# Layer 1's experts: a branch on TensorE to products that work on 32 slots, for experts with 32 tokens or fewer

## The chip, the cores and the metric

The kernel runs on one core of a Trainium2 chip. The metric is the device time of one execution in microseconds; less is better. A core has TensorE (PE in the profile, and PEld for its weight loads), VectorE (DVE), ScalarE (ACT), GpSimd (POOL), SyncE (SP, which issues most DMAs) and 16 DMA engines. They run beside each other and wait for each other by semaphores.

## The reference, cut to what matters

The model has two layers. Each mixes 256 latent tokens with 256 context tokens (attention beside a linear recurrence), and then sends tokens through 16 experts, of which a router picks two for each token. In layer 1, the last, only the 256 latent tokens go through the experts, so an expert has 32 tokens on average.

```python
D_MODEL = 1024
N_EXPERTS = 16
TOP_K = 2
D_EXPERT = 512
...
def grouped_moe(h, router_w, router_b, w_gate, w_up, w_down):
    ...
    out = jnp.zeros_like(h)
    for e in range(N_EXPERTS):
        hid = jax.nn.silu(h @ w_gate[e]) * (h @ w_up[e])
        out = out + combine[:, e:e + 1] * (hid @ w_down[e])
    return out
```

Everything is fp32. Each expert has three weights of 2048 KB (gate and up 1024 x 512, down 512 x 1024), and each layer has weights of its own.

## The kernel before

Layer 0's experts (`experts`) give every expert 64 slots, and up to three extra blocks of 32 slots each that PE and GpSimd reach through branches on the expert's token count (`extras`, line 1572). The products of an extra block (`upx`, `downx`) have 128x32 stationary operands and 256 moving columns, four beside each other in the array; their PSUM tiles are `ccg` and `ccd`.

Layer 1's experts (`experts_last`) have no extra blocks: every expert works on 64 slots, whatever its count, and tokens beyond 64 would go through a loop behind the stage (`more`). `route` puts each token's rank within its expert into `rk`. For an expert e these steps follow each other:

- `one_hot_f` (DVE, line 1723) compares ranks with slot numbers and makes a 0/1 matrix of tokens by slots, for two experts at a time.
- `gat0` (PE, tile `pgx`): products of the tokens with these matrices gather the two experts' tokens, transposed, into `xT`.
- `up` (PE, tile `pgu`): gate goes to partitions 0 to 63, up to partitions 64 to 127, 8 products of 512 columns each. Two beside each other fill the array's 128 columns.
- `gated`: ACT makes silu of gate, DVE multiplies by up (tile `hid`).
- `hturn` (PE, tile `phd`) turns `hid`, ACT copies it out.
- `down` (PE, tile `pdn`): 8 products of 512 columns, the two halves of the output beside each other.
- `gain` and `halves` (DVE, ACT) scale the result and split it into two parts for the return; `oturn` (PE, tile `poh`) turns the 0/1 matrix.
- `back` (PE, tile `pcb`, and DVE): four products bring the slots back to tokens, and DVE adds them into `xtok` with the combine weight.

The order on each engine is written out by hand in `step` and run as written (`manual_schedule`): up of expert e + 1, down of e, and back of e - 1 between their parts. The pieces of up and of back are interleaved: after the fifth and sixth of the eight steps of up comes one back, after the last another, and the same within down.

The weights come through SP's queue (`load`, line 216) into eight buffers of 2048 KB, so 2 2/3 experts fit. The loads are issued in the order gate, up, down, expert by expert, and each waits until PE has done the last product that reads the buffer it takes. Gate and up have 16 KB of one partition in one run in memory, and so has layer 1's down; layer 0's down has four runs of 4 KB. Expert 15's gate and up are loaded in two halves each.

One fp32 product is two records on PE in the trace. All products stand at line 114 (`mm`), so they are told apart by their tiles.

Of the kernel before, what the change touches and what calls it, by code (L numbers as in the profile page):

```python
# [108 lines left out]
def backbone(ctx: ExitStack, tc: tile.TileContext, a: dict):  # L109
# [99 lines left out]
    def part(l, e, i, pl=None):  # L209
        n_, k = (("gate", 8), ("up", 8), ("down", 4))[i]  # L210
        t = wchunk(f"w{n_[0]}{l}_{e}", pl).rearrange("p (k n) -> p k n", k=k)

        return t, a[f"exp_w_{n_}"][l, e].rearrange("(k p) n -> p k n" if i == 2 and l == 0 else "(p k) n -> p k n", k=k)
# [1060 lines left out]
    def route(l, lg, Q, R):  # L1274
# [72 lines left out]
        if last:  # L1347
            return
# [361 lines left out]
    def experts_last(l, tmp, h2k, ahead, after):  # L1710


        r = rt_all[l]
        rk, oi, wc = r["rk"], r["oi"], r["wc"]
        xt, hid, hidT, oh, ohT, hl, W = {}, {}, {}, {}, {}, {}, {}
        it = C("iota")[:, 0:64]

        def one_hot_f(es, rks):

            o = tmp.tile([P, 2, 2, 64], F32, name="ohf", tag="ohf", bufs=3)  # L1720
            for i, e in enumerate(es):
                for t in range(2):
                    dve.tensor_scalar(o[:, i, t, :], it, rks[i][t], None, op0=OP.is_equal)
                oh[e] = o, i

# [14 lines left out]
        def up(ps, x, w, ks):  # L1740
            for k in ks:
                mm(ps[0:64, :], x[:, k, :], w[0][:, k, :], k == 0, k == KC - 1)
                mm(ps[64:128, :], x[:, k, :], w[1][:, k, :], k == 0, k == KC - 1)

        def gated(ps):
# [3 lines left out]
            dve.tensor_tensor(h.rearrange("s k p -> s p k"), sg.rearrange("s (p k) -> s p k", k=4),  # L1749
                              ps[64:128, :].rearrange("s (p k) -> s p k", k=4), op=OP.mult)  # L1750
            return h
# [9 lines left out]
        def down(ps, h, w, ks=range(4)):  # L1761
            for k in ks:
                for q in range(2):
                    mm(ps[64 * q:64 * q + 64, :], h[:, k, :], w[2][:, k, q * 512:(q + 1) * 512], k == 0, k == 3)

# [35 lines left out]
        def step(e):  # L1801
# [22 lines left out]
        def more():  # L1824
# [3 lines left out]
            with tc.If(anyv > 0, preferred_fallthrough_block=False):  # L1828
                for e in range(NE):
                    ov = nc.values_load(oi[0:1, e:e + 1], min_val=0, max_val=8)  # L1830
                    with tc.If(ov > 0, preferred_fallthrough_block=False):
# [5 lines left out]
                        with tc.For_i(0, ov, 1):  # L1837
                            rb = tmp.tile([P, 2], F32, name="rbg", tag="rbg", bufs=1)
                            dve.tensor_scalar(rb[:], rk[:, :, e], base[:, 0:1], None, op0=OP.subtract)
                            one_hot_f((e,), [[rb[:, t:t + 1] for t in range(2)]])  # L1840
                            gat0((e,))
                            ps = psb("pgu", "mm")
                            up(ps, xt[e], w, range(KC))
# [15 lines left out]
        with tc.manual_schedule(engines=ORDERED):  # L1859
# [11 lines left out]
            pu, pd = psb("pgu", "mm"), psb("pdn", "mm")  # L1871
# [4 lines left out]
            for i in range(3):  # L1876
                up(pu, xt[e], W[e], ((0, 1, 2, 3, 4), (5, 6), (7,))[i])
                if i < 2:
                    back2(e - 2, i)
            hid[e] = gated(pu)  # L1880
            for i in range(2):
                down(pd, hidT[e - 1], W[e - 1], (2 * i, 2 * i + 1))
                back2(e - 2, 2 + i)
# [3 lines left out]
            pd = psb("pdn", "mm")  # L1887
            down(pd, hidT[e], W[e])
# [11 lines left out]
    MOE = dict(mm=2, tr=2), dict(mm=3, tr=3, cb=2)  # L1900
# [124 lines left out]
```

## Time and profile before

| | |
|---|---|
| median of 3 runs | 1109.69 us (1105.55 to 1113.52) |
| the profiled execution, its own time | 1107.49 us |
| its span in the profile | 1105.6 us |
| PE busy | 984.8 us, 89% |
| DVE busy | 600.5 us, 54% |
| ACT busy | 432.3 us, 39% |
| POOL busy | 195.7 us, 18% |
| DMA, mean rate over the span | 270 GB/s |
| first and last pgu products of layer 1 | 843.6 and 1073.4 us |

The profile is one execution. The span goes from the first to the last instruction; the execution's own time is 1.9 us longer. Times in rows are microseconds from the span's start unless marked ns. Busy time of PE counts matmuls in the array; PEq and PEld are its queue and its weight loads. "x <- y" in a row of waits means that x waited for y.

### The profile page before, as it was taken

How to read it: one execution, taken by the hardware profiler on the slowest of the kernel's cores; microseconds unless marked ns; L12 is line 12 of the kernel's file. 1: busy time of each engine (PE TensorE's matmuls, PEld its weight loads, DVE VectorE, ACT ScalarE, POOL GpSimd, SP SyncE). 2: the span in 40 equal slices, each digit the busy share in tenths (PEclk: the TensorE clock that was granted, in tenths of full speed). 3: DMA queues.
4: the chain of work that ended last, by engine and by line, in shares of the span. 5: the costliest groups of instructions: out<-in, count | busy, mean ns of one | idle time of the engine just before them, and what ended most of it. 6: DMA issues, size and time to landing. Idle time of an engine off the chain costs nothing. (4 is left out here: it accounts for less than half of the span.)

```text
span 1105.6 us, 15540 instructions
## 1 busy us (share of the span) xinstructions
PE 984.8 (89%) x5791; PEld 520.2 (47%) x5791; DVE 600.5 (54%) x1363; ACT 432.3 (39%) x858; POOL 195.7 (18%) x208
## 2 busy tenths in 40 slices
PE   5999999899589989999898599897977999999993
PEld 3555465678444434333332366353765434444431
DVE  3567487686743325534433356679863344444445
ACT  3635678465511212212221264796741122221222
POOL 2000033331544313212110200205241000000000
PEclk9999999899669989999998799998997999999996
DMA  9947674011866876999997565558156799999941
GB/s 381 396 167 299 229 272 186 30 39 58 323 244 259 286 287 190 398 407 410 395 397 305 155 268 188 200 180 305 49 210 270 317 421 413 429 400 416 397 197 41
DMA packets 51963, 298.87 MB, mean 270 GB/s; under 512 B 5457, under 2 KB 8401, under 8 KB 35969
## 3 DMA queue, kind: packets, MB, share of 16 engines
q1 hardware_dynamic: 44800, 279.88, 64.1%
q0 software_dynamic: 6896, 16.87, 5.4%
q8 instruction: 73, 1.20, 0.4%
q10 hardware_dynamic: 144, 0.52, 0.1%
q14 instruction: 50, 0.40, 0.1%
HBM read 288.86 MB, written 10.49 MB: 271 GB/s over the span
## 5 line engine op out<-in xcount | busy, mean ns | idle before, releaser
L114 PE MATMUL pdn<-wd,hidT 128*64 128x512 f32 x512 | 124.3, 619 | 5.3 <-PEq L1572 4.0
L114 PE MATMUL pgu<-wg,xgT 128*64 128x512 f32 x256 | 118.7, 617 | 0.3 <-issue 0.3
L114 PE MATMUL pgu<-wu,xgT 128*64 128x512 f32 x256 | 118.7, 617 | 0.2 <-DMA wu<-exp_w_up_dram 0.2
L114 PE MATMUL pgu<-wu,xT 128*64 128x512 f32 x256 | 116.5, 598 | 0.0
L114 PE MATMUL pgu<-wg,xT 128*64 128x512 f32 x256 | 116.5, 598 | 0.0
L1795 DVE SCALAR_TENSOR_TENSOR xtok<-pcb,wc,xtok 128x512 f32<-128x512 f32 x64 | 47.7, 750 | 102.7 <-PE pcb L114 102.7
L1455 DVE TENSOR_TENSOR hid<-hid,pgu 64x512 f32<-64x512 f32 x16 | 11.0, 690 | 126.2 <-ACT hid L1454 126.2
L114 PE MATMUL pproj<-hh,wps 128*128 128x512 f32 x288 | 76.9, 407 | 0.0
L846 POOL TENSOR_TENSOR wo<-wf,wo 128x512 fp32r<-128x512 f32 x29 | 41.0, 1434 | 201.9 <-ACT wo L844 170.1
L1430 POOL DMA_INDIRECT yd<-xtok,sgs x24 | 38.6, 1608 | 185.0 <-DVE xtok L1489 183.5
L114 PEld LDWEIGHTS pdn<-wd,hidT 128*64 128x64 f32 x512 | 34.7, 140 | 67.5 <-issue 66.8
L114 PEld LDWEIGHTS pgu<-wg,xgT 128*64 128x64 f32 x256 | 34.8, 142 | 65.2 <-issue 64.7
L114 PEld LDWEIGHTS pproj<-hh,wps 128*128 128x128 f32 x288 | 53.2, 188 | 19.6 <-issue 6.5
L114 PEld LDWEIGHTS pgu<-wg,xT 128*64 128x64 f32 x256 | 32.5, 136 | 61.6 <-issue 60.7
L1454 ACT ACTIVATE hid<-pgu 64x512 f32<-64x512 f32 x16 | 9.4, 590 | 104.8 <-PE pgu L114 104.7
L1954 POOL TENSOR_TENSOR fin<-xtok,fin 128x512 f32<-128x512 f32 x2 | 2.5, 1278 | 254.8 <-DVE xtok L1795 254.8
L1748 ACT ACTIVATE hid<-pgu 64x512 f32<-64x512 f32 x16 | 9.4, 589 | 94.6 <-PE pgu L114 94.5
L795 ACT ACTIVATE Pm<-psc,mx,qy 128x512 f32<-128x512 f32 (+1 forms) x48 | 33.5, 703 | 21.3 <-DVE mx L789 21.1
L497 DVE TENSOR_TENSOR wps<-win,wps 128x512 fp32r<-128x512 f32 x48 | 32.6, 687 | 14.9 <-ACT wps L496 14.4
L114 PE MATMUL pproj<-hT,wps 128*128 128x512 f32 x144 | 39.8, 397 | 0.0
L114 PEld LDWEIGHTS pgu<-wu,xgT 128*64 128x64 f32 x256 | 34.8, 142 | 6.9 <-issue 5.2
L114 PE MATMUL pwa<-wo,mh 128*128 128x512 f32 x128 | 36.3, 407 | 1.6 <-POOL wo L846 0.9
(442 smaller groups left out, 2079.5 us busy)
## 6 DMA issues: line engine op xcount, KB each, us to landing
wd<-exp_w_down_dram SPq DMA_DIRECT2D x31, 2048.0 KB, 14.2
wu<-exp_w_up_dram SPq DMA_DIRECT2D x27, 2048.0 KB, 9.6
wg<-exp_w_gate_dram SPq DMA_DIRECT2D x27, 2048.0 KB, 15.9
xtok<-ada_w_dram SPq DMA_DIRECT2D x7, 2048.0 KB, 7.4
win<-w_in_dram SPq DMA_DIRECT2D x6, 2048.0 KB, 16.2
adac<-ada_w_dram SPq DMA_DIRECT2D x5, 2048.0 KB, 8.0
xtok<-ada_w_dram SPq DMA_DIRECT2D x8, 1024.0 KB, 5.1
adac<-ada_w_dram SPq DMA_DIRECT2D x8, 1024.0 KB, 4.9
```

Source lines behind the costliest of these rows:

```text
L114: pe.matmul(out, lhsT, rhs, start=start, stop=stop)
L497: dve.tensor_tensor(wl, wv, wh.bitcast(F32), op=OP.subtract)
L795: act.activation(ps[h], sc_[i][h], AF.Exp, bias=mx[:, h:h + 1], scale=qr[:, ti, j, h:h + 1], accum_out=sm[:, h:h + 1])
L846: pool.tensor_tensor(lo, w, hi.bitcast(F32), op=OP.subtract)
L1430: st = pool.indirect_dma_start(out=dst, out_offset=bass.IndirectOffsetOnAxis(ap=idx, axis=0), in_=y, in_offset=None, bounds_check=dst.shap ...
L1454: mark.append(act.activation(sg, ps[0:64, :], AF.Silu).ins.name)
L1455: dve.tensor_tensor(h.rearrange("s k p -> s (k p)"), sg, ps[64:128, :], op=OP.mult)
L1748: act.activation(sg, ps[0:64, :], AF.Silu)
L1795: dve.scalar_tensor_tensor(x, cb, wc[:, t, e:e + 1], x, op0=OP.mult, op1=OP.add)
L1954: (dve if q else pool).tensor_tensor(fin["t"][:, 1 + t, cs], x, fin["t"][:, 0, cs], op=OP.mult)
```

## The change

- `route` makes, for layer 1, a flag for every expert that is 1 when it has over 32 tokens (`big`, and as an integer `bigi`): two small DVE operations.
- `one_hot_f` compares ranks with slot numbers chosen by the flag: 1 to 64 for a big expert, and 1 to 32 twice for another, so that each of its tokens has two slots, s and s + 32. One more DVE operation for each expert, two at the start of the stage (`its`).
- `either` loads the flag into a register of PE (once for an expert) and branches, for up and for down. Only PE branches.
- The other arm of up (`up_half`) multiplies 32 slots by 256 columns, four products beside each other: the first and second half of gate, the first and second half of up. A token's first 256 hidden values then stand in slot s, the other 256 in slot s + 32.
- The other arm of down (`down_half`) sums over 256 hidden values for each slot, so that a token's result is the sum of its two slots; `back` adds them, as the 0/1 matrix has both.
- For that, the down weights of layer 1 have the row order of layer 0's (runs of 4 KB), and `gated` writes in plain order.
- All of up now stands in one tile, `pgu`, with one buffer, cleared once by ACT; the four `back` of an expert are no longer between the parts of up and of down but behind each.

```diff
@@ part
-        return t, a[f"exp_w_{n_}"][l, e].rearrange("(k p) n -> p k n" if i == 2 and l == 0 else "(p k) n -> p k n", k=k)
+        return t, a[f"exp_w_{n_}"][l, e].rearrange("(k p) n -> p k n" if i == 2 else "(p k) n -> p k n", k=k)
@@ route
         if last:
+
+            big = rt_all[l]["big"] = R.tile([P, NE], F32, name="big", tag="big", bufs=1)
+            bigi = rt_all[l]["bigi"] = R.tile([P, NE], I32, name="bigi", tag="bigi", bufs=1)
+            dve.tensor_scalar(big[:], cnt[:], 0.5 * NB, None, op0=OP.is_gt)
+            dve.tensor_copy(bigi[:], big[:])
             return
@@ experts_last
+        its = tmp.tile([P, 2, 64], F32, name="its")
+        dve.tensor_scalar(its[:, 0], C("iota")[:, 128:192], float(NB), None, op0=OP.subtract)
+        dve.tensor_tensor(its[:, 1], it, its[:, 0], op=OP.subtract)
+
+        def one_hot_f(es, rks, own=True):
 
             o = tmp.tile([P, 2, 2, 64], F32, name="ohf", tag="ohf", bufs=3)
             for i, e in enumerate(es):
+                ie = it
+                if own:
+                    ie = tmp.tile([P, 64], F32, name="ite", tag="ite", bufs=2)[:]
+                    dve.scalar_tensor_tensor(ie, its[:, 1], big[:, e:e + 1], its[:, 0], op0=OP.mult, op1=OP.add)
                 for t in range(2):
-                    dve.tensor_scalar(o[:, i, t, :], it, rks[i][t], None, op0=OP.is_equal)
+                    dve.tensor_scalar(o[:, i, t, :], ie, rks[i][t], None, op0=OP.is_equal)
                 oh[e] = o, i
+
+        def either(e, whole, half):
+
+            if e not in bv:
+                bv[e] = nc.values_load(bigi[0:1, e:e + 1], engines=[PEe], min_val=0, max_val=1)
+            with tc.If(bv[e] > 0, preferred_fallthrough_block=False) as c:
+                whole()
+            with c.Else():
+                half()
...
+        def up_half(ps, x, w):
+
+            for k in range(KC):
+                for m in range(2):
+                    for q in range(2):
+                        mm(ps[64 * m + 32 * q:64 * m + 32 * q + 32, 0:256], x[:, k, 0:32], w[m][:, k, 256 * q:256 * q + 256],
+                           k == 0, k == KC - 1)
...
+        def down_half(ps, h, w):
+
+            for k in range(2):
+                for q in range(2):
+                    for i in range(2):
+                        mm(ps[64 * q + 32 * i:64 * q + 32 * i + 32, :], h[:, k, 32 * i:32 * i + 32],
+                           w[2][:, 2 * i + k, q * 512:(q + 1) * 512], k == 0, k == 1)
+
+        pgu = psb("pgu", "gu")
+        act.activation(pgu, C("iota"), AF.Copy, scale=0.0)
+
+        def ups(e):
+            ps = pgu
+            either(e, lambda: up(ps, xt[e], W[e]), lambda: up_half(ps, xt[e], W[e]))
+            return ps
...
@@ step
-            pu = psb("pgu", "mm")
-            for i in range(3):
-                up(pu, xt[e + 1], W[e + 1], ((0, 1, 2, 3), (4, 5), (6, 7))[i])
-                if e >= 1 and i:
-                    back(e - 1, 0, i - 1)
-            hid[e + 1] = gated(pu)
+            hid[e + 1] = gated(ups(e + 1))
+            if e >= 1:
+                for i in range(2):
+                    back(e - 1, 0, i)
             if e >= 0:
-                pd = psb("pdn", "mm")
+                pd = downs(e)
+            if e >= 1:
                 for i in range(2):
-                    down(pd, hidT[e], W[e], range(2 * i, 2 * i + 2))
-                    if e >= 1:
-                        back(e - 1, 1, i)
+                    back(e - 1, 1, i)
```

The last expert's order is changed in the same way, and the PSUM buffers from three that `pgu` and `pdn` share to two for `pdn` and one for `pgu`.

## Rows read from the trace of the kernel before

**Rows 1.** Page, part 2: DMA share in tenths and GB/s, 40 slices.

```profile
DMA  9947674011866876999997565558156799999941
GB/s 381 396 167 299 229 272 186 30 39 58 323 244 259 286 287 190 398 407 410 395 397 305 155 268 188 200 180 305 49 210 270 317 421 413 429 400 416 397 197 41
```

**Rows 2.** Windows: us, busy us of each engine, PEclk, DMA share, GB/s.

```profile
851.00:861.00 10.00, 7.25 (x44) 6.21 (x46) 1.71 (x2) 2.58 (x4) 0.00 (x0) 0.83 0.94 374
861.00:872.00 11.00, 11.00 (x56) 3.70 (x54) 1.75 (x2) 2.08 (x5) 0.00 (x0) 1.00 0.51 186
872.00:1063.00 191.00, 191.00 (x929) 76.32 (x927) 84.43 (x132) 39.57 (x81) 0.00 (x0) 1.00 0.99 411
1063.00:1064.00 1.00, 1.00 (x6) 0.29 (x4) 0.56 (x1) 0.00 (x0) 0.00 (x0) 1.00 0.54 221
```

**Rows 3.** Timeline of PE: start us, us, engine, line, operation, count.

```profile
859.53 0.64 PE L114 MATMUL pgu<-wg,xT 128*64 128x512 f32 x1
...
866.45 3.60 PE L114 MATMUL pdn<-wd,hidT 128*64 128x512 f32 x16
...
887.64 0.64 PE L114 MATMUL pgu<-wg,xT 128*64 128x512 f32 x1
...
917.92 0.64 PE L114 MATMUL pgu<-wg,xT 128*64 128x512 f32 x1
```

**Rows 4.** Waits of SP's queue, 780:1106: us in total, times, longest us.

```profile
SPq L216 <- PE pgu L114: 105.7, 9, 15.8
SPq L216 <- PE pdn L114: 93.1, 13, 12.9
```

**Rows 5.** Windows of two stretches with the load queue full.

```profile
572.80:582.00 9.20, 8.40 (x50) 3.67 (x48) 5.11 (x10) 2.73 (x6) 1.55 (x1) 1.00 1.02 411
922.00:937.00 15.00, 15.00 (x66) 4.63 (x61) 6.76 (x12) 2.89 (x6) 0.00 (x0) 1.00 1.01 431
```

**Rows 6.** Timeline of PE near the end.

```profile
1052.37 0.64 PE L114 MATMUL pgu<-wg,xT 128*64 128x512 f32 x1
...
1079.34 3.65 PE L114 MATMUL pdn<-wd,hidT 128*64 128x512 f32 x16
```

**Rows 7.** Groups by form, PE, 300:640: count | busy us, mean ns.

```profile
L114 PE MATMUL ccg<-wu,xxT 128*32 128x256 f32 x256 | 28.6, 380 | 0.0
...
L114 PE MATMUL ccd<-wd,hixT 128*32 128x256 f32 x256 | 14.8, 381 | 0.0
```

**Rows 8.** Line 1572: durations in ns min/median/max, first and last start us.

```profile
L1572 PEldq COMPARE_BRANCH  x66: 69/218/3558, 323.5 to 615.9; - x66
```

**Rows 9.** Waits of PE, 300:620: us in total, times, longest us.

```profile
PE pslot L114 <- PEq L1572: 4.2, 10, 0.7
...
PE phd L1461 <- PEq L1572: 3.8, 7, 0.7
```

**Rows 10.** Line 1828, columns as in rows 8.

```profile
L1828 PEldq COMPARE_BRANCH  x2: 84/1910/3736, 1089.9 to 1090.6; - x2
```

**Rows 11.** Timeline of DVE before layer 1's experts.

```profile
837.77 0.73 DVE L1723 TENSOR_SCALAR ohf<-cst,rk 128x64 f32<-128x64 f32 x4
```

**Rows 12.** Timeline of PE; in brackets the idle us before, and its releaser.

```profile
838.44 5.19 PE L114 MATMUL pgx<-ohf,h2k 128*128 128x128 f32 x32 [1.12 <-DVE ohf L1723]
...
853.75 0.46 PE L1756 MATMUL phd<-ident,hid 64*128 64x64 f32 x4 [3.10 <-DVE hid L1749]
854.13 5.47 PE L114 MATMUL pgx<-ohf,h2k 128*128 128x128 f32 x32
...
883.97 3.74 PE L114 MATMUL pgx<-ohf,h2k 128*128 128x128 f32 x32
```

**Rows 13.** Timeline of SP's queue: issues of weight loads.

```profile
850.67 0.33 SPq L216 DMA_DIRECT2D wd<-exp_w_down_dram  x1
...
866.64 0.33 SPq L216 DMA_DIRECT2D wu<-exp_w_up_dram  x1
```

**Rows 14.** Window after the idle time at 853, columns as in rows 2.

```profile
855.00:858.40 3.40, 3.40 (x18) 3.40 (x17) 0.69 (x1) 0.00 (x0) 0.00 (x0) 0.50 1.00 429
```

More of the change, by code (lines that the diff above doesn't have):

```diff
@@ L1738, in gat0, with up @@
                 xt[e] = x[:, :, 64 * i:64 * i + 64]
-        def up(ps, x, w, ks):
-            for k in ks:
+        def up(ps, x, w):
+            for k in range(KC):
                 mm(ps[0:64, :], x[:, k, :], w[0][:, k, :], k == 0, k == KC - 1)
                 mm(ps[64:128, :], x[:, k, :], w[1][:, k, :], k == 0, k == KC - 1)
+        def up_half(ps, x, w):
+            for k in range(KC):
+                for m in range(2):
+                    for q in range(2):
+                        mm(ps[64 * m + 32 * q:64 * m + 32 * q + 32, 0:256], x[:, k, 0:32], w[m][:, k, 256 * q:256 * q + 256],
+                           k == 0, k == KC - 1)
         def gated(ps):
@@ L1748, in gated @@
             act.activation(sg, ps[0:64, :], AF.Silu)
-            dve.tensor_tensor(h.rearrange("s k p -> s p k"), sg.rearrange("s (p k) -> s p k", k=4),
-                              ps[64:128, :].rearrange("s (p k) -> s p k", k=4), op=OP.mult)
+            dve.tensor_tensor(h.rearrange("s k p -> s (k p)"), sg, ps[64:128, :], op=OP.mult)
             return h
@@ L1759, in hturn, with down, downs @@
             return o
-        def down(ps, h, w, ks=range(4)):
-            for k in ks:
+        def down(ps, h, w):
+            for k in range(4):
                 for q in range(2):
                     mm(ps[64 * q:64 * q + 64, :], h[:, k, :], w[2][:, k, q * 512:(q + 1) * 512], k == 0, k == 3)
+        def down_half(ps, h, w):
[10 more added lines that the diff above has]
+            return ps
+        def downs(e):
+            ps = psb("pdn", "mm")
+            either(e, lambda: down(ps, hidT[e], W[e]), lambda: down_half(ps, hidT[e], W[e]))
+            return ps
         def gain(ps):
@@ L1839, in more @@
                             dve.tensor_scalar(rb[:], rk[:, :, e], base[:, 0:1], None, op0=OP.subtract)
-                            one_hot_f((e,), [[rb[:, t:t + 1] for t in range(2)]])
+                            one_hot_f((e,), [[rb[:, t:t + 1] for t in range(2)]], False)
                             gat0((e,))
                             ps = psb("pgu", "mm")
-                            up(ps, xt[e], w, range(KC))
+                            up(ps, xt[e], w)
                             h = hturn(gated(ps))
@@ L1870, in experts_last @@
             e = NE - 1
-            pu, pd = psb("pgu", "mm"), psb("pdn", "mm")
             def back2(e, i):
                 back(e, i % 2, i // 2)
[L1876 to L1880, printed above, removed]
+            hid[e] = gated(ups(e))
             for i in range(2):
-                down(pd, hidT[e - 1], W[e - 1], (2 * i, 2 * i + 1))
-                back2(e - 2, 2 + i)
+                back2(e - 2, i)
+            pd = downs(e - 1)
+            for i in range(2, 4):
+                back2(e - 2, i)
             hidT[e] = hturn(hid[e])
@@ L1886, in experts_last @@
             ohT[e - 1], ohT[e] = oturn(e - 1), oturn(e)
-            pd = psb("pdn", "mm")
-            down(pd, hidT[e], W[e])
+            pd = downs(e)
             y = gain(pd)
@@ L1899, in backbone @@
     MIX = dict(mm=2, tr=2, sc=3, ada=1)
-    MOE = dict(mm=2, tr=2), dict(mm=3, tr=3, cb=2)
+    MOE = dict(mm=2, tr=2), dict(mm=2, gu=1, tr=3, cb=2)
     pst = ExitStack()
```

5 lines of the change are left out of this document (3 added, 2 removed).

## The prediction

> **What bounds the kernel now.** I read the slices of the page first. In slices 33 to 38 (884 to 1050 us) the DMA row stands at 9, with 397 to 429 GB/s, as it does in layer 0's experts in slices 17 to 21 [rows 1]. The stage by windows comes next [rows 2]: from 872 to 1063 us the 16 DMA engines have a share of 0.99 and move 411 GB/s, and PE is busy for 191.00 of 191 us. Two resources are full at once, so neither busy share says which of them sets the pace. The reader should see that these are the same pace told twice. One expert is three weights of 2.097 MB, so 6.29 MB at 411 GB/s is 15.3 us; two experts on PE take 917.92 - 887.64 = 30.28 us [rows 3], that is 15.14 us each. Who leads is told by the waits of SP's queue [rows 4]: the loads wait for PE's products to give buffers back, 105.7 us for pgu and 93.1 us for pdn; no product of this stretch waits for a load. So PE leads, but with how little room? In a stretch with several loads queued the DMA moved 431 GB/s at a share of 1.01 [rows 5], one weight in 2.097 / 0.431 = 4.87 us, an expert in 14.6 us. PE at 15.14 us is 0.5 us per expert from a second bound.
>
> That is the main point: a faster PE stage gains little in the steady state. It may gain in two other places. At the start the loads wait long for PE (861 to 872 moves 186 GB/s [rows 2]). At the end PE is behind: the bytes stop in the window 1063 to 1064 [rows 2], while the last pdn products end at 1079.34 + 3.65 = 1082.99 [rows 6]. These 19.5 us, and the 22.6 us from there to the end of the span at 1105.6, lie behind the DMA.
>
> **Which experts take the short arm.** Working the reference's inputs through its router gives, for the 256 tokens of layer 1, 33 28 53 54 17 7 19 17 12 32 24 46 32 15 63 60 tokens for experts 0 to 15: ten experts (1, 4 to 10, 12, 13) have 32 or fewer, and none has more than 64. The same count for layer 0 asks for eight blocks of extra slots, and the trace has eight: 256 records on wu, 32 to a block [rows 7], which supports the list.
>
> **The change, part by part.** *The products.* A whole up runs from 859.53 to 866.45, 6.9 us, a whole down 3.6 us [rows 3]. The short up has the shape of layer 0's extra block (four 128x32 by 256 products beside each other): 28.6 us for eight blocks, 3.6 us each. The extra block's down took 14.8 / 8 = 1.85 us [rows 7]; the new down has 512 columns in half as many products, so as many columns in all. An expert saves 6.9 - 3.6 + 3.6 - 1.8 = 5.1 us, ten save 51 us of PE. PE then needs on average 15.14 - 51 / 16 = 11.9 us per expert, under the 14.6 us that the DMA needs: the bound changes hands, and most of the 51 us turns into waiting for weights.
>
> *The branches.* PE gets 16 register loads and 32 compare-and-branches. Layer 0 has 66 on PE, 0.07 to 3.56 us long, median 0.22 [rows 8]; PE's idle time put down to them stands in three rows of the waits, 4.2, 4.0 and 3.8 us, 12.0 us in 22 places (the first and the last: [rows 9]). That is 0.18 us over all and 0.55 us where it shows, because the queue runs ahead of the array. I take 0.4 us; ends 0.07 and 3.7 us, the latter from the jump over the overflow code at the kernel's end [rows 10]. While PE waits for weights these cost nothing; in the first and the last steps each counts.
>
> *The down weights' rows.* 16 KB runs become four runs of 4 KB. Layer 0 loads pieces with 4 KB runs; where nearly nothing else is queued they move 411 GB/s at a share of 1.02 [rows 5], 5.10 us for a weight instead of 4.87: 0.24 us. Fourteen of the last 40 loads (wd of experts 2 to 15) are such: 3.3 us. Ends: 0, and the 15 us that all 40 would lose at 400 GB/s (rival 1).
>
> *The front.* Before the first gather products stand six new small DVE operations (big, bigi, two of its, two ite) of about 0.18 us, as the four ohf took 0.73 us [rows 11]: 1.1 us, and PE waits for ohf already there (1.12 us [rows 12]). With one register load and branch 1.5 us; ends 0.8 (the branch hidden behind the gather products, the operations in part behind PE's rank products) and 5 (a branch of 3.7 us). It counts in full, since the loads wait for up(0).
>
> *What costs nothing.* Zeroing pgu is one ACT operation while ACT is idle. pgu's single buffer adds no wait: the turn of hid already waits for the product that reads it, and stands ahead of the next up. Back's products now stand two beside each other behind up and behind down; the two pcb buffers take a pair, and DVE is busy for 84.43 of 191 us [rows 2], which also covers the ite operations. If that cover fails, a back waits for one DVE operation more per expert, inside PE's new waiting time. SP issues the same loads in the same order.
>
> **The sum, along the DMA.** After 850.67 [rows 13] 40 loads are left (wd of expert 2, three each for 3 to 15): 83.9 MB, 194.6 us at 431 GB/s. Before, the stage lost against that rate 10 x (1 - 374/431) = 1.3 us, 11 x (1 - 186/431) = 6.3 us and 191 x (1 - 411/431) = 8.9 us, together 16.5 us [rows 2]. After: the first 1.3 us stay. The 6.3 us wait for up(1), then for down(0): wu of expert 3 is issued at 866.64, right behind up(1) [rows 13]; up(1) is short (28 tokens) and ends 3.3 us earlier less a branch, so 3.2 us stay. The 8.9 us come from a queue that runs dry because PE gives buffers back late; with PE ahead I leave 1.0 us for the next load, which waits for down(1). Add 3.3 us for 4 KB rows and 1.5 us for the front: 10.3 us, 6.2 us less. The last weight lands at 1063.5 - 6.2 = 1057.3.
>
> **And the tail behind it.** Experts 14 and 15 have 63 and 60 tokens and stay whole. Behind wu of expert 14 come its wd (5.1 us), gate and up of 15 (9.7 us) and wd of 15 (5.1 us), so up(14) can start at 1057.3 - 19.9 = 1037.4. From there PE is not held: the second half of wu of 15 lands at 1052.2 and is needed later than that. In before this chain runs from 1052.37 to 1082.99, 30.6 us [rows 6]. Short down(13) takes off 1.8 us, four branches add 1.6 us. Between the up products of 13 and 14 PE has about 8 us of work in 14.8 us, so it idles for some 6 us, and its clock will be at the lower level when it starts. The trace shows that price: after PE's 3.1 us of idle time that end at 853.75, the window 855 to 858.4 has a granted clock of 0.50, 1.2 instead of 2.4 GHz [rows 14], and the gather products took 5.47 us where they take 3.74: 1.7 us [rows 12]. So 30.6 - 1.8 + 1.6 + 1.7 = 32.1 us, to 1069.5, plus the unchanged 22.6 us: 1092.1 us, 13.5 us less. The profiled execution took 1107.49 us, so it would take 1094; the median of the runs is 2.2 us above it, and 1109.69 - 13.5 = 1096 us is my forecast. Its own range is 1089 to 1103.
>
> The Trainium skill bears on the ceiling that this sum uses. "DMA: Bandwidth & Descriptors", Specifications, has a fabric ceiling of 435 GB/s and an HBM limit of about 358 GB/s per core. The trace agrees with the first (431) and contradicts the second: at 358 GB/s the 40 loads would take 234 us, 40 us more than in my sum, and the stage of before could not have been as it was. By the first nothing over 1% is left above my rate.
>
> **Rivals.** *1. The DMA gets no faster.* Layer 0's full slices, with 4 KB rows and its gathers and scatters, move 395 to 410 GB/s [rows 1], not 431. At 400 the 40 loads take 209.8 us, 15.2 us lost instead of 3.3: the end is 11.9 us later, 1108 us. Against it: layer 1 has no gathers from memory, and the piece-wise stretch gave 411. Chance 0.14, no change.
>
> *2. The branches become the bound (slower).* If each of the two branches per expert goes to code that is not at hand, as the one that took 3.74 us [rows 10], PE needs 11.9 + 7.5 = 19.4 us per expert, 4.2 us more than now: about 68 us slower, 1177 us. It decides from (15.14 - 11.9) / 2 = 1.6 us per branch. For it: new arms without prefetch hints. Against: 66 branches in layer 0, some over longer code, have a median of 0.22 us [rows 8]. The Trainium skill, "Runtime: NRT & Kernel Launch", Instruction fetch mechanics, says that a taken branch out of the window fetched ahead stalls for a fetch; the 3.74 us agrees, the median says it is rare. Chance 0.08, of which 0.05 slower.
>
> *3. The clock.* Where PE waits for weights once per expert, it may run much of its time at 1.2 GHz. As long as it recovers as before 859.53, where up(1) runs at its usual 6.9 us [rows 3], 1.7 us per expert vanish in the idle time. If the last 30 us ran wholly at the lower level, they would take almost twice as long, some 25 us more: 1121 us; from 13.5 us lost there the gain is gone. The Trainium skill, "TensorE: Matmul & The Clock Gate", HAM oscillation, describes a kernel of thin products waiting for DMA that fell back at every tile; here each burst is 8 us or longer. Chance 0.06, slower.
>
> *4. More than forecast.* No 4 KB loss, no clock loss, cheap branches: 3.3 + 1.7 + 2 us more, about 1089 us; with the front at its lower end 1088. Chance 0.10. That the full 51 us arrive would take 6.29 MB in 11.9 us, 528 GB/s, which no stretch shows; 0.
>
> *5. It doesn't do what it says.* If counts on the chip sent the experts to the whole arm, PE would lead as now, with 0.8 us more per expert and the front: 1109.69 + 12.8 + 1.1, about 1124 us. Two experts sit at 32 and one at 33, but these alone change nothing. Chance 0.02.
>
> **How the numbers follow.** Forecast 0.60, of which 0.50 under 1098.6 us and 0.10 above. A difference of 1%, 11 us, is about what a measurement of this kernel can tell from no change. Faster: 0.50 + 0.10 = 0.60; no change: 0.10 + 0.14 + 0.03 = 0.27; slower: 0.05 + 0.06 + 0.02 = 0.13. The range reaches from just under rival 4 to just over rival 1: 1086 to 1109; 0.13 and the fast end's last few per cent lie outside.
>
> **What would show it.** Right: PE busy in the stage falls to about 80% with idle time that ends on DMA of wu; SP's waits for pgu and pdn shrink while DMA stays near 1.0 at 420 GB/s or more; bytes end near 1057; PE ends under 13 us behind them instead of 19.5; PEclk falls at each wait. Wrong: PE's idle time ends on its own queue (branches), the wd loads take over 5.3 us each in a full queue, or up(0) ends more than 3 us later.

## The result and the profile after

The changed kernel takes 1096.87 us (median of 4 runs, 1092.16 to 1098.52), the kernel before beside it 1107.93 us: a ratio of 0.9897, 95% interval 0.9867 to 0.9927. The forecast was 1096. The profiled execution took 1097.18 us, its span 1095.4; forecast for it was 1094. The total came out right, but several of the terms behind it did not, as the rows show.

Below, "the stage" runs from the issue of wu of expert 0 to the end of the span. What stands ahead of it differs by several us from one execution to the next (the stage begins between 811 and 823 us), so positions of two kernels are compared from the stage's start. It is at 815.22 in before and at 816.31 after; the stage took 290.4 and 279.1 us.

After, page, part 2:

```profile
PEclk9899999899759999999999899998996899889886
DMA  9937675010856876999999384638328599999981
GB/s 381 402 156 288 229 283 208 30 40 39 319 214 271 269 279 210 374 413 414 393 393 387 105 340 154 229 114 326 110 86 328 216 423 425 422 421 426 426 336 42
```

After, windows (columns as in [rows 2]):

```profile
855.90:862.70 6.80, 6.57 (x32) 6.46 (x33) 0.86 (x2) 0.37 (x1) 0.00 (x0) 0.50 1.05 436
861.00:872.00 11.00, 11.00 (x104) 6.07 (x105) 1.63 (x3) 2.14 (x5) 0.00 (x0) 0.92 0.48 174
872.00:1040.00 168.00, 144.08 (x1176) 70.50 (x1172) 78.28 (x140) 39.53 (x81) 0.00 (x0) 0.91 1.01 422
1040.00:1047.00 7.00, 3.25 (x9) 0.99 (x10) 0.31 (x1) 0.00 (x0) 0.00 (x0) 0.52 1.00 413
1064.00:1065.00 1.00, 1.00 (x6) 0.34 (x6) 0.62 (x1) 0.35 (x1) 0.00 (x0) 1.00 0.16 66
```

The bound has changed hands, as [rows 2] has its counterpart: PE was busy for 191 of 191 us and is busy for 144 of 168, at a granted clock of 0.91 instead of 1.00; the DMA moves 422 instead of 411 GB/s. But the start is not better. The window 861 to 872 moves 174 GB/s where it moved 186, and the bytes end at about 1064.4 (the window 1064 to 1065 has a share of 0.16), where they ended at about 1063.5 before [rows 2], not at 1057.

After, waits of PE from 840 us on, then of SP's queue from 780 on:

```profile
PE pgu L114 <- DMA wu<-exp_w_up_dram: 20.9, 7, 4.1
PE pgu L114 <- DMA wg<-exp_w_gate_dram: 4.5, 2, 2.8
PE phd L1789 <- DVE hid L1783: 2.8, 1, 2.8
...
SPq L216 <- PE pdn L114: 133.4, 13, 16.3
SPq L216 <- PE pgu L114: 17.4, 1, 17.4
```

PE now waits for weights, 25.4 us in nine places, and nowhere for its own queue, where the branches are. SP's waits did not shrink as forecast. Those for pgu fell from 105.7 to 17.4 us, but those for pdn rose from 93.1 to 133.4 [rows 4]: of the loads that wait for PE, all but one now wait for a down.

After, the branches of layer 1's arms (columns as in [rows 8]):

```profile
L1747 PEldq COMPARE_BRANCH  x52: 64/177/354, 843.5 to 1066.6; - x52
```

After, timeline of SP's queue and then of PE:

```profile
853.31 0.38 SPq L216 DMA_DIRECT2D wd<-exp_w_down_dram  x1
...
870.64 0.33 SPq L216 DMA_DIRECT2D wu<-exp_w_up_dram  x1
...
840.83 5.44 PE L114 MATMUL pgx<-ohf,h2k 128*128 128x128 f32 x32 [2.05 <-DVE ohf L1738]
846.20 0.64 PE L114 MATMUL pgu<-wg,xT 128*64 128x512 f32 x1
...
856.74 6.68 PE L114 MATMUL pgx<-ohf,h2k 128*128 128x128 f32 x32
863.35 0.41 PE L114 MATMUL pgu<-wg,xT 128*32 128x256 f32 x2
...
866.94 3.65 PE L114 MATMUL pdn<-wd,hidT 128*64 128x512 f32 x16
...
1043.84 1.11 PE L114 MATMUL pgu<-wu,xT 128*64 128x512 f32 x1 [3.75 <-DMA wu<-exp_w_up_dram]
...
1053.09 1.92 PE L114 MATMUL pdn<-wd,hidT 128*32 128x512 f32 x16
...
1069.46 3.65 PE L114 MATMUL pdn<-wd,hidT 128*64 128x512 f32 x16
```

Here is the start. The short up(1) runs from 863.35 to 866.94, 3.6 us as forecast. The load of wu of expert 3 does not go out behind it, as it did in [rows 13], but at 870.64, when down(0) has ended (866.94 + 3.65). And here is the end: the last product ends at 1069.46 + 3.65 = 1073.1, 8.7 us behind the last bytes, where it was 19.5.

So the gain lies in two places, and mostly in the second. The load of wu of expert 3 goes out 2.9 us later in the stage (54.3 against 51.4). From there until only the last expert's 6.3 MB are left to land it takes 177.3 instead of 181.2 us, 3.9 us less. From that mark to the end of the last down it takes 25.2 instead of 35.2 us, 10.0 us less. Together the last down ends 256.8 us into the stage instead of 267.8. What follows it is nearly the same: 22.6 us before, 22.3 after.

### The profile page after: what moved, and what is told of

It reads as the page before. It is cut to its first block, busy times and chain, and to the rows that moved or that the text cites. A ratio compares the mean times of both kernels' runs of the same rounds, so it can differ in the third digit from the quotient of the medians.

```text
span 1095.4 us, 16290 instructions
## 1 busy us (share of the span) xinstructions
PE 943.6 (86%) x6111; PEld 519.8 (47%) x6111; DVE 597.9 (55%) x1383; ACT 432.0 (39%) x859; POOL 196.1 (18%) x208
## 5 line engine op out<-in xcount | busy, mean ns | idle before, releaser
L114 PE MATMUL pgu<-wu,xT 128*32 128x256 f32 (+1 forms) x416 | 89.5, 486 | 20.9 <-DMA wu<-exp_w_up_dram 20.9
L114 PE MATMUL pdn<-wd,hidT 128*64 128x512 f32 (+1 forms) x512 | 101.7, 606 | 5.0 <-PEq L1577 3.0
L114 PE MATMUL pgu<-wg,xT 128*32 128x256 f32 (+1 forms) x416 | 92.0, 491 | 6.7 <-DMA wg<-exp_w_gate_dram 4.5
L1460 DVE TENSOR_TENSOR hid<-hid,pgu 64x512 f32<-64x512 f32 x16 | 11.0, 690 | 126.0 <-ACT hid L1459 126.0
L1783 DVE TENSOR_TENSOR hid<-hid,pgu 64x512 f32<-64x512 f32 x16 | 11.0, 690 | 106.4 <-ACT hid L1782 106.3
L114 PEld LDWEIGHTS pdn<-wd,hidT 128*64 128x64 f32 (+1 forms) x512 | 28.7, 130 | 60.1 <-issue 56.9
L114 PEld LDWEIGHTS pgu<-wu,xT 128*32 128x32 f32 (+1 forms) x416 | 33.7, 131 | 48.9 <-DMA wu<-exp_w_up_dram 26.4
L1850 DVE SCALAR_TENSOR_TENSOR xtok<-pcb,wc,xtok 128x512 f32<-128x512 f32 x64 | 45.1, 746 | 9.1 <-PE pcb L114 7.4
L114 PEld LDWEIGHTS pgu<-wg,xT 128*32 128x32 f32 (+1 forms) x416 | 33.1, 131 | 30.2 <-issue 17.0
```

The source lines that it names most:

```text
L114: pe.matmul(out, lhsT, rhs, start=start, stop=stop)
L1460: dve.tensor_tensor(h.rearrange("s k p -> s (k p)"), sg, ps[64:128, :], op=OP.mult)
L1783: dve.tensor_tensor(h.rearrange("s k p -> s (k p)"), sg, ps[64:128, :], op=OP.mult)
L1850: dve.scalar_tensor_tensor(x, cb, wc[:, t, e:e + 1], x, op0=OP.mult, op1=OP.add)
```

## The experiments

All ratios are to the kernel before, run beside each kernel. In the table "wu 3" is the issue of wu of expert 3, "35 loads" the time from there until 6.3 MB of the weights are left (counted from the packets of the trace: the 35 loads from wu of expert 3 to wd of expert 14 and what is still on its way of the load ahead of them, 74.0 MB, but 74.6 in e6 and 74.5 in e11), "last down" the end of the last pdn product, all from the stage's start in the profiled execution, in us.

| kernel | ratio, 95% interval | wu 3 | 35 loads | last down | stage |
|---|---|---|---|---|---|
| before | 1 | 51.4 | 181.2 | 267.8 | 290.4 |
| the change | 0.9897 (0.9867 to 0.9927) | 54.3 | 177.3 | 256.8 | 279.1 |
| e7, the change again | 0.9913 (0.9883 to 0.9943) | 51.2 | 177.2 | 254.4 | 276.5 |
| e1, free order | 0.9898 (0.9874 to 0.9922) | 51.3 | 177.3 | 253.7 | 276.2 |
| e2, fixed arms | 0.9875 (0.9849 to 0.9902) | 51.3 | 176.7 | 253.6 | 276.6 |
| e3, arms of 12 and 13 | 0.9912 (0.9882 to 0.9943) | 51.8 | 177.4 | 253.9 | 277.1 |
| e4, 16 KB runs | 0.9905 (0.9878 to 0.9931) | 54.6 | 175.5 | 256.3 | 278.4 |
| e5, order alone | 0.9911 (0.9879 to 0.9943) | 51.6 | 176.8 | 258.2 | 281.0 |
| e6, arms in old order | 0.9891 (0.9848 to 0.9934) | 47.7 | 178.4 | 253.0 | 275.6 |
| e8, free order, 16 KB runs | 0.9881 (0.9850 to 0.9912) | 52.1 | 175.6 | 254.0 | 276.9 |
| e9, dummy products | 0.9901 (0.9866 to 0.9936) | 52.1 | 177.2 | 255.9 | 278.9 |
| e10, e8 and e9 together | 0.9852 (0.9819 to 0.9885) | 49.8 | 175.6 | 251.3 | 273.7 |
| e11, e10, arms of 1, 12, 13 alone | 0.9804 (0.9761 to 0.9846) | 48.8 | 175.2 | 247.9 | 271.2 |
| e12, e11 without arms | 0.9935 (0.9908 to 0.9963) | 50.6 | 174.6 | 259.2 | 282.7 |

**e7: the change once more.** It is told first, since it says how much of a difference counts.

> The changed kernel once more, to stand beside the three others on the same chip: 0.990 to the kernel before. Nothing is told apart by it alone; its profiled execution shows how far the stage (from the issue of wu of expert 0 to the end of the span, 279.1 us in the first profile) differs between two executions: 0.5 us or less, if the differences of 2 to 3 us of the earlier runs in this stage are to count.

The stage took 276.5 us, not 279.1: the same kernel differs by 2.6 us. By the condition set, differences of 2 to 3 us between single stages do not count alone, and below an experiment is judged by its waits and steps as well. Where the 2.6 us come from can be seen on PE in e7:

```profile
858.95 3.84 PE L114 MATMUL pgx<-ohf,h2k 128*128 128x128 f32 x32
```

The gather products behind PE's wait for hid took 3.84 us here and 6.68 above, where the window 855.9 to 862.7 has a granted clock of 0.50. The wait ahead of them is the same 2.8 us both times; in one execution the clock had fallen to 1.2 GHz behind it, in the other not (in e7 the window 858.1 to 864.9 has a granted clock of 1.00).

**e1: buffers in the order in which they come free.** The eight weight buffers are the same in both kernels, but the compiled programs hand them out in another order. Before, wu of expert 3 takes the buffer of gate 1, free after up(1). In the changed kernel it takes that of down 0, and wd of expert 3 takes gate 1's.

```diff
-                    W[e + 2] = load_expert(l, e + 2, (4,) if e == NE - 3 else ())
+                    W[e + 2] = reload_expert(e + 2, (4,) if e == NE - 3 else ())
...
+        def reload_expert(e, cuts):
+            old = (W[0][1] if e == 3 else W[e - 4][2]), W[e - 2][0], W[e - 2][1]
...
-        with tc.manual_schedule(engines=ORDERED):
+        with tc.manual_schedule(engines=ORDERED | {mybir.EngineType.SP}):
```

Gate, up and down of an expert take the tiles listed in `old`, so tiles in the trace keep older names.

> The changed kernel (1096.9 us), with every load of layer 1's experts 3 to 15 given the weight buffer that comes free first (up of expert 3 takes the buffer of gate 1, not that of down 0), in program order. Theory (the 4 us at the start of the stage are lost because the load of wu of expert 3 waits for down(0) instead of up(1), and the DMA sets the pace from there to the last weight): that load is issued at about 867.0 instead of 870.6, the last weight lands 3 to 4 us earlier, near 1061, and the time is about 1093.3 us. Rival (the loads' own rate in the steady stretch takes it back, or PE holds them again): the load is issued earlier, the last weight still lands at 1064, and the time stays at 1097 us.

e1, timeline of SP's queue and PE:

```profile
857.26 0.45 SPq L216 DMA_DIRECT2D wu<-exp_w_gate_dram  x1
870.28 0.33 SPq L216 DMA_DIRECT2D wg<-exp_w_up_dram  x1
...
860.22 6.43 PE L114 MATMUL pgx<-ohf,h2k 128*128 128x128 f32 x32
870.17 3.65 PE L114 MATMUL pdn<-wd,hidT 128*64 128x512 f32 x16
```

The load goes out at 870.28, as down(0) starts, so its wait is up(1)'s and not down(0)'s: 3.5 us earlier than it would be behind down(0), with gather products as slow as in the first profile of the change. From there the 35 loads take the same 177.3 us and the stage ends 2.9 us earlier. The mechanism is shown; its worth is not, since the median ratio did not move (0.9898) and e7 reached the same stage by its clock.

**e2: arms fixed in the source.**

```diff
-            if e not in bv:
-                bv[e] = nc.values_load(bigi[0:1, e:e + 1], engines=[PEe], min_val=0, max_val=1)
-            with tc.If(bv[e] > 0, preferred_fallthrough_block=False) as c:
-                whole()
-            with c.Else():
-                half()
+            (whole if e in (0, 2, 3, 11, 14, 15) else half)()
```

> The changed kernel with the arms fixed in the source by the known counts: no register loads and no branches on TensorE, the same products. It leaves out the choice at run time. Theory (the branches cost nothing that shows, but their presence changed the order in which weight buffers are handed out): buffers go out as before, wu of expert 3 is issued right behind up(1) near 867, and the time is that of the kernel with the free order, about 1093 us, give or take 1 us. Rival 1 (a branch costs 0.4 us wherever PE is on the path, as forecast): another 2.4 us less, 1091 us. Rival 2 (the order of the buffers has nothing to do with the branches): wu of expert 3 still at 870.6 and 1095 to 1097 us.

e2, timeline of SP's queue and PE:

```profile
869.77 0.33 SPq L216 DMA_DIRECT2D wu<-exp_w_up_dram  x1
873.37 0.38 SPq L216 DMA_DIRECT2D wd<-exp_w_down_dram  x1
...
869.67 3.65 PE L114 MATMUL pdn<-wd,hidT 128*64 128x512 f32 x16
```

Without branches wu goes out behind up(1) again and wd behind down(0): taking the branches out of this program gives back the order of before. Rival 2 falls. But branches alone don't decide it: e6 below has five of them for an expert and the order of before. What in the program decides which buffer a load gets stays open. With wu sent out as early as in e1 the stage is 276.6 against 276.2. The 2.4 us that branches at 0.4 us would cost in the first and last steps lie within what e7 leaves open between two stages; that they cost nothing that shows rests on the rows of waits, where no idle time of PE ends on its queue.

**e3: arms for experts 12 and 13 alone.**

```diff
+            if e not in (12, 13):
+                return whole()
             if e not in bv:
```

> The changed kernel with the choice of the arm at experts 12 and 13 only; all others take the whole arm without a branch, so PE does 8 x 5.1 = 41 us more products. Theory (the DMA sets the pace in the steady stretch, and the change gains only in PE's lag behind the last weight): the last weight lands at 1064 to 1065, PE ends 8 to 10 us behind it, and the time is 1096 to 1099 us. Rival (each short expert brings its share of the 11 us): two tenths of it, 1105.7 us.

0.9912, the same as with ten arms. The theory's number holds, but its reason was incomplete. With whole arms PE should need 15.14 us for an expert and lead again. e3, timeline of PE, and then three rows of the kernel before:

```profile
889.30 0.64 PE L114 MATMUL pgu<-wg,xT 128*64 128x512 f32 x1
...
895.79 0.59 PE L114 MATMUL pgu<-wg,xT 128*64 128x512 f32 x1
...
896.32 0.73 PE L114 MATMUL pcb<-hl,ohT 128*128 128x512 f32 x2
896.98 3.65 PE L114 MATMUL pdn<-wd,hidT 128*64 128x512 f32 x16
...
918.18 0.64 PE L114 MATMUL pgu<-wg,xT 128*64 128x512 f32 x1
```

```profile
892.41 0.59 PE L114 MATMUL pgu<-wg,xT 128*64 128x512 f32 x1
...
892.94 0.51 PE L114 MATMUL pcb<-hl,ohT 128*128 128x512 f32 x1
893.37 0.64 PE L114 MATMUL pgu<-wg,xT 128*64 128x512 f32 x1
```

Two whole experts take 918.18 - 889.30 = 28.88 us, 14.44 each. The products of up follow each other in 0.43 us. A back is one record, as its operands are fp32r. So a lone back takes 893.37 - 892.84 = 0.53 us out of the row, and a pair 896.98 - 896.22 = 0.76, 0.38 each. With the first up behind a lone back 0.05 slower, four lone backs cost about 0.7 us more per expert than two pairs. The forecast had put the new order of back among the things that cost nothing. It gains, and it takes the whole arm below the 14.6 us of the forecast for the DMA.

**e5: the new order alone**, in the kernel before.

```diff
-            for i in range(3):
-                up(pu, xt[e + 1], W[e + 1], ((0, 1, 2, 3), (4, 5), (6, 7))[i])
-                if e >= 1 and i:
-                    back(e - 1, 0, i - 1)
+            up(pu, xt[e + 1], W[e + 1], range(KC))
             hid[e + 1] = gated(pu)
+            if e >= 1:
+                for i in range(2):
+                    back(e - 1, 0, i)
```

Down and the last expert likewise.

> The kernel before with one part of the change: the four back of an expert stand two beside each other behind up and behind down, no longer between their parts. No short arms, no branches, 16 KB runs, buffers as before. In the run with two short experts two whole experts took 14.44 us each on PE, where the kernel before takes 15.14; that is below the 14.6 us that the DMA needs. Theory (the order alone brings PE's whole arms down to the pace of the DMA): 13 experts x 0.7 us = 9 us less, up to the 11 us of the whole change: a ratio of 0.990 to 0.992 to the kernel before. Rival (the forecast: the order costs and gives nothing, the short arms give it all): 1.000.

0.9911: this line-up of products alone gives what the change gives. e5, window from wu of expert 3 on:

```profile
863.01:1039.80 176.79, 176.79 (x906) 74.89 (x903) 78.22 (x126) 38.71 (x79) 0.00 (x0) 1.00 1.00 420
```

PE is busy for all of it and no product waits for a weight, so PE leads still, with the DMA's share at 1.00 beside it. It is 9.4 us faster over the stage: 13 experts x 0.7 us is 9.1.

**e6: the arms in the old order.**

```diff
-        def ups(e):
-            ps = pgu
-            either(e, lambda: up(ps, xt[e], W[e]), lambda: up_half(ps, xt[e], W[e]))
-            return ps
+        def ups(e, cuts, f=None):
+            for i, ks in enumerate(cuts):
+                either(e, lambda: up(pgu, xt[e], W[e], ks), lambda: up_half(pgu, xt[e], W[e], ks))
+                if f:
+                    f(i)
+            return pgu
```

> The changed kernel with the order of before: back stands between the parts of up and of down, and the arm is chosen for each part (five branches for an expert in place of two). PE then needs 11.9 + 0.7 us for an expert on average, still well under the DMA's 14.6. Theory (PE only has to get under the pace of the DMA, and either part of the change does that, so the parts don't add up): again 0.988 to 0.992 to the kernel before. Rival 1 (the gains add up, and the order brings 9 of the 11 us): 0.998. Rival 2 (branches on the path at 0.4 us each): three more for each of the first and last steps, some 3 us above the changed kernel, 0.993.

0.9891. Arms alone, order alone and both give the same within the intervals. If they added up, both would be at 0.980, and the change's interval ends at 0.987. e6, the branches:

```profile
L1747 PEldq COMPARE_BRANCH  x130: 64/176/367, 844.4 to 1065.6; - x130
```

130 records in place of 52, and again no idle time of PE ends on them. Here wu of expert 3 goes out right behind up(1), as before, and the gather products ran at full clock (3.84 us), which explains the 47.7; the 178.4 has 0.6 MB more in it than the others, some 1.5 us.

**e4: runs of 16 KB with short arms.**

```diff
-                        mm(ps[64 * m + 32 * q:64 * m + 32 * q + 32, 0:256], x[:, k, 0:32], w[m][:, k, 256 * q:256 * q + 256],
-                           k == 0, k == KC - 1)
+                        mm(ps[64 * m + 32 * q:64 * m + 32 * q + 32, :].rearrange("s (p k) -> s p k", k=4)[:, :, 0:2], x[:, k, 0:32],
+                           w[m][:, k, :].rearrange("p (c k) -> p c k", k=4)[:, :, 2 * q:2 * q + 2], k == 0, k == KC - 1)
```

> The changed kernel with the down weights read in runs of 16 KB as before; the short arm takes hidden columns in pairs (a strided moving operand), so that each slot has the hidden values of its rows of the down weight, and the product after silu is written in turned order as before. Theory of the forecast (a down weight in 4 KB runs takes 5.10 instead of 4.87 us): the last weight lands 3 us earlier and the time is about 1093.6 us. Rival (the length of the runs doesn't matter in a full queue): 1097 us and 5.0 us per weight as now. Should the strided operand slow the short up beyond its 3.6 us, this is seen in its products' durations, and while PE waits for weights it costs nothing.

The 35 loads, twelve of them down weights, take 175.5 instead of 177.3 us, and 175.2 to 175.6 in the other kernels with 16 KB runs and short arms (e8, e10, e11). That is 1.8 / 12 = 0.15 us a weight, where 0.24 was forecast. The time did not fall by the 3 us of the theory: the stage is 0.7 us shorter, and the ratio did not move measurably.

**e8: e1 and e4 together**, on the same lines: `reload_expert` with the down weights in

```diff
-"(k p) n -> p k n"
+"(p k) n -> p k n"
```

> The changed kernel with the buffers in the order in which they come free and the 16 KB runs of the down weights together, all ten short arms kept. Theory (both shorten the DMA's stretch in layer 1, by 2.9 and 0.7 to 1.5 us in the stages of the earlier runs): the stage takes 274.7 to 275.5 us instead of 279.1, and the ratio to the kernel before is 0.986. Rival (both are lost again before the end): stage 279, ratio 0.990.

0.9881 and 276.9 us, between the two: the loads' term came (175.6), the start's was eaten by gather products at half clock (6.43 us).

**e9: dummy products in two of PE's waits.**

```diff
+            if e + 1 == NE - 2:
+                warm(ident, 9)
             hid[e + 1] = gated(ups(e + 1))
...
+            if e < 0:
+                warm(ident, 5)
             hidT[e + 1] = hturn(hid.pop(e + 1))
```

> The changed kernel with dummy products in two of PE's waits: 5 behind up(0), where PE waits 2.8 us for hid, and 9 ahead of up(14), where it waits for wg and wu. In two executions of the changed kernel the stage (from the issue of wu of expert 0 to the end of the span) took 279.1 and 276.5 us; in the first the gather products behind up(0) ran at half clock (6.7 us), in the second not (3.8 us). Theory (what is left of the start and of the end chain hangs on the clock after PE's waits): gather products at 3.8 us, no half clock behind the wu of expert 14, a stage of 274.5 to 275.5 us, ratio to the kernel before 0.986 to 0.988. Rival (the clock falls all the same, or the dummies hold up the products behind them): 276.5 to 279 us, 0.990.

e9, timeline of PE, and a window:

```profile
849.77 1.38 PE L114 MATMUL warm<-ident 128*128 128x128 f32 x10
...
853.07 3.84 PE L114 MATMUL pgx<-ohf,h2k 128*128 128x128 f32 x32
...
1030.25 2.17 PE L114 MATMUL warm<-ident 128*128 128x128 f32 x18
...
1037.27 1.11 PE L114 MATMUL pgu<-wu,xT 128*64 128x512 f32 x1 [3.73 <-DMA wu<-exp_w_up_dram]
```

```profile
1036.30:1043.10 6.80, 5.83 (x14) 1.71 (x16) 0.00 (x0) 0.00 (x0) 0.00 (x0) 0.50 1.02 419
```

A miss. The gather products ran at 3.84 us, but e7 had that without dummies. Ahead of up(14) the dummies stood in the wrong place: the wait that counts, 3.73 us for wu, lies behind the first gate product of up(14), where they can't reach, and the clock fell as before. The question whether dummies hold the clock stays open. The start of the other profiles leans to yes: in the ten without dummies the gather products behind up(0) took 3.84 us twice, about 5.5 three times and 6.4 to 6.7 five times; in the four with dummies (e9 to e12) 3.84 us three times and 5.47 once.

**e10 and e11: all of it, with ten arms and with three.** e10 has the edits of e8 and e9; e11 also

```diff
+            if e not in (1, 12, 13):
+                return whole()
             if e not in bv:
```

> The changed kernel with the buffers in the order in which they come free, 16 KB runs, and the dummy products in the two waits. With the first two alone the stage took 276.9 us, with gather products at half clock. Theory (the terms are those of a chain and add up: 3.5 us of the load that waits for down(0), 1.7 us of runs, 4 us of clock, against 279.1 us): 271 to 273.5 us, ratio 0.983 to 0.985. Rival (one of them hides the others): 275 us or more, 0.988.

> The kernel with free order, 16 KB runs and dummy products, with the choice of the arm at experts 1, 12 and 13 only; the seven others of the ten short ones take the whole arm without a branch (36 us more products on PE). Theory (the arms in the middle of the stage only turn PE's work into waits, since the DMA sets the pace, and the whole arm in the new order needs 14.44 us against 14.6): the same stage as with all ten, within 1 us, 271 to 274 us, ratio 0.983 to 0.986. Rival (each arm brings its share of about 0.7 us): 5 us longer, 0.988.

e10, then e11, windows from wu of expert 3 on:

```profile
870.74:1046.30 175.56, 153.85 (x1232) 77.03 (x1234) 84.50 (x142) 41.05 (x84) 0.00 (x0) 0.92 1.00 424
```

```profile
860.74:1035.90 175.16, 174.51 (x1012) 77.25 (x1014) 81.81 (x132) 41.04 (x84) 0.00 (x0) 1.00 1.00 425
```

In e10 the terms came in part: 273.7 us, 5.4 of the 9.2 us of the theory less than 279.1, just above its range, and 0.9852. The clock's term is the one that is mostly missing: the gather products took 5.47 us, where 3.84 was hoped for, and up(14) ran at the lower clock still. e11, the best kernel of the study, has seven arms fewer and is not slower, at 0.9804. The two intervals overlap a little, and by e7 the 2.5 us between the two stages do not count alone; but the two kernels ran side by side on one chip, and five of the six times of e11 (1083.1 to 1089.8 us, the sixth 1093.8) lie below all six of e10 (1090.3 to 1096.4). The reader should compare the two rows: the DMA moves 424 and 425 GB/s; PE works 154 us at a clock of 0.92 in the one and 174.5 us at 1.00 in the other. In the middle the short arms buy idle time only, and with the idle time comes a lower clock. e10, then e11, up(14) in the timeline of PE:

```profile
1042.36 8.78 PE L114 MATMUL pgu<-wd,xT 128*64 128x512 f32 x30 [3.11 <-DMA wd<-exp_w_up_dram]
```

```profile
1031.72 7.09 PE L114 MATMUL pgu<-wd,xT 128*64 128x512 f32 x32
```

In e10 up(14) waits for wu and takes 8.8 us behind the wait; in e11 no product of layer 1's experts waits for a weight, and it takes 7.1. That is 1.7 of the 3.4 us by which the last down ends earlier in e11; 1.0 us is there at wu 3 already: PE waits 0.5 us less for DVE ahead of the first gather products (1.59 instead of 2.05 us), and the two groups of gather products took 10.4 instead of 10.9 us. That the clock is what makes e11 faster is so shown for 1.7 us in one execution of each, and supported by the granted clock over the whole span, 0.935 to 0.947 in the six runs of e11 and 0.923 to 0.932 in those of e10.

**e12: e11 without arms.**

```diff
-            if e not in (1, 12, 13):
+            if e not in ():
                 return whole()
```

> The kernel with three short arms (ratio 0.980, stage 271.2 us) without any: all experts take the whole arm, no branch; new order, free order, 16 KB runs and dummy products stay. Theory (the arm of expert 1 brings 3.3 us at the start, those of 12 and 13 bring the 5 to 6 us by which PE ended later behind the loads with the order alone): a stage of 279 to 281 us, ratio 0.988. Rival (order, buffers, runs and dummies bring it all, since PE at 14.44 us keeps up with the loads): 271 to 273 us, 0.980 to 0.982.

0.9935, the stage 282.7: the three arms are worth 11.5 us there, somewhat more than the theory's 279 to 281 and 0.988. The loads reach their 6.3 MB mark at the same pace (174.6), but the last down ends 34.0 us behind that mark instead of 23.9. In e11 up(14) starts 219.8 us into the stage, here 230.0: with every arm whole PE leads again, as in e5, and no product waits for a weight. e12, timeline of PE:

```profile
1047.74 2.17 PE L114 MATMUL warm<-ident 128*128 128x128 f32 x18
1049.85 7.09 PE L114 MATMUL pgu<-wd,xT 128*64 128x512 f32 x32
```

The dummies ahead of up(14) stand on the path of a leading PE and take their 2.1 us, about what this stage is longer than with the order alone (e5, 281.0 us and 0.9911): with PE leading, free order and 16 KB runs brought nothing. How the 11.5 us divide among the arms was not tried. With the new order alone, arms at 12 and 13 brought 3.9 us in one profile (e3 against e5) and nothing in the ratio (0.9912 and 0.9911).

## Why the prediction was right, and where it wasn't

- *The bound changes hands* (PE 15.14 us, DMA 14.6): right. PE waits for wu and wg, the DMA's share is 1.01. The 35 loads from wu of expert 3 on got 3.9 us shorter; 8.9 - 1.0 - 3.3 = 4.6 was forecast. The room was smaller than the 0.5 us per expert of the forecast, whose 431 GB/s come from 15 us [rows 5]: over 175 us the DMA moved at most 425 GB/s (e11, e12), 6.29 / 0.425 = 14.8 us per expert.
- *"What costs nothing: back's products now stand two beside each other"*: wrong, and the largest miss. That the move could gain was not asked, though the trace had the price of a lone back (0.53 us; a pair of the new order takes 0.38 each). The order takes 9.4 us off alone (e5). The total survived because the change's parts don't add: both only have to bring PE under the DMA's pace. "It doesn't do what it says", rival 5, would therefore not have cost 14 us; with whole arms throughout, e5 and e12 gained 0.9 and 0.65%.
- *The start* ("wu of expert 3 is issued right behind up(1)", "SP issues the same loads in the same order"): wrong. The order of loads is the same, that of their buffers is not, and the load waited for down(0) and went out 3.7 us behind up(1) where it went out 0.2 behind it before: 3.5 us. The gather products at 1.2 GHz took 6.68 us where before took 5.47 [rows 12], another 1.2. With the front's 1.5 us (forecast, and measured: up(0) starts 29.9 us into the stage instead of 28.3) and 3.3 less for the short up(1) this makes 2.9 us later; 1.6 us earlier was forecast. This term, 4.5 us, is most of why the bytes did not end 6.2 us earlier but at the same place in the stage.
- *4 KB runs*, 0.24 us a weight: 0.15 (e4), a term of 2.1 us instead of 3.3. The DMA's rate with them was 420, without them 424 GB/s; rival 1's 400 was not seen in this stretch.
- *Branches*, 0.4 us where they show: no idle time of PE ends on one (e6, and the changed kernel), and without them (e2) the time is not measurably less. The front's 1.5 us is there, and mostly from its DVE operations: the first gather products start 24.5 us into the stage instead of 23.2. On the jump, the Trainium skill, "Runtime: NRT & Kernel Launch", Instruction fetch mechanics, expects a stall where the target is out of the fetched window; no branch of these arms took over 0.37 us, in 182 records of two kernels.
- *The end chain*, 32.1 us from up(14): 1073.1 - 1043.84 = 29.3. Down(13) at 1.92 us and the half clock until 1047 came as forecast; the four branches' 1.6 us did not, and the two steps with grouped backs would take off some 1.4 us more (2 x 0.7, an estimate from e3).
- *The sum*: the loads end 7 us later than forecast (1064.4 against 1057.3; 1.1 us of it is the later start of the stage), the chain behind them is 3.5 us shorter (8.7 behind the last bytes instead of 12.2). The forecast had 6.2 us of the gain from earlier bytes and 7.3 from PE's lag behind them; in fact nearly all of it, 10.8 us, is the lag. The forecast for the profiled execution was 3 us too low, that for the median 1 us; the rest is the spread of the medians. The right total came by luck in part, from terms whose errors partly cancel.
- *Rival 3, the clock*: right as a mechanism, small in price. The clock is 0.91 in the stretch and costs 1.6 us at the end (up(14) takes 8.7 us behind its wait, 7.1 without one) and up to 2.8 at the start. The Trainium skill, "TensorE: Matmul & The Clock Gate", HAM oscillation, describes a kernel whose clock falls back at each wait for the DMA. The granted clocks of after and e10 in the stretch (0.91 and 0.92, with waits for weights) against that of e11 (1.00, without) show the same on a smaller scale, and e11 points to a cure here: leave PE the work that fills the waits.

## What to carry to other kernels

Where two resources run at nearly the same pace, several edits that relieve the one can be worth about as much as the first of them: test each alone before keeping all, here a branch-free reordering of four products beside ten branches. Here, work taken off PE paid where PE is last, at the start and behind the last load (arms of experts 1, 12 and 13), and with the work left in the middle TensorE's clock stayed up. Price a move of instructions from both sides, and after an edit look at what each load waits for, since a change elsewhere in the program can change which buffer it gets.

## What the runs showed of the hardware beyond that

- A lone 128x512 product (fp32r, one record) between 64-column pairs of fp32 took 0.53 us out of the row, two beside each other 0.76.
- The same program had its gather products at 3.84 us in one execution and at 6.68 in another, behind the same wait of 2.84 us.
- Moving operands in pairs of elements with gaps and PSUM writes in the same pattern (e4, e8) left the short up at 3.8 us, 0.15 us more than the plain one (48.23 to 52.05 us into the stage in e8, 47.57 to 51.24 in e1).
